# Loads of the later adaLN modulations: from SyncE's queue to GpSimd's, two tiles ahead of their sums, as one chain

## The chip, the cores and the metric

The kernel runs on one core of a Trainium2 chip. The metric is the device time of one execution in microseconds (us); a comparison goes by the median of several executions. Engines: PE is TensorE, DVE is VectorE, ACT is ScalarE, POOL is GpSimd, SP is SyncE, which here issues the transfers and computes nothing.

## The reference, cut to what matters

Two layers over x of 256 tokens and 2048 channels. A layer has a token mixer (a convolution module in layer 0, stick-breaking attention in layer 1) and then a gated feed-forward (ConvFFN) with 5632 hidden channels. Each of the four sub-layers has its own modulation from the conditioning vector c:

```python
def ada_ln(c, w, b):
    mod = jax.nn.silu(c) @ w + b
    shift, scale, gate = jnp.split(mod, 3, axis=-1)
...
shift, scale, gate = ada_ln(c, ffn_mod_w[i], ffn_mod_b[i])
h = rms_norm(x, ffn_norm_g[i]) * (1.0 + scale) + shift
x = x + gate * conv_ffn(h, ffn_up_w[i], ffn_dw_w[i], ffn_dw_b[i], ffn_down_w[i])
```

One modulation is a product of a vector with a 2048 x 6144 matrix, 48 MB of float32. Called by their names in the kernel they are mix0, ffn0 (layer 0), mix1 and ffn1 (layer 1). All is float32, and the output is the final RMS norm.

## The kernel before, in words

**Matrix products.** The weights come as a stream of raw tiles of 128 x 1024 float32 (512 KB, eight blocks of 128 x 128; the prediction calls one a piece), in the order in which TensorE uses them. ScalarE rounds a tile to its high half `wh`, VectorE subtracts to get the low half `wl` (`split_next`, lines 226 to 243), and TensorE makes three matmuls per block: wh with xh, wh with xl, wl with xh (lines 288 to 290). `raw` has 6 buffers, `wh` and `wl` 4 each. Raw tiles are loaded up to 5 pieces ahead, halves made up to 3 ahead (`look`).

**Order of the stages.** After the convolution module (pw1, pw2: 32 split pieces) the first ffn has the products up00a, up00b, up01a, down00, up01b and down01 with 8, 80, 4, 44, 84 and 44 pieces. Numbered through, the subtractions of pw2 are 1 to 32, up00a 33 to 40, up00b 41 to 120, up01a 121 to 124, down00 125 to 168, up01b 169 to 252, down01 253 to 296. Then come the attention's q, k and v products, the o product and the second ffn with the same products (688 pieces in all).

**Modulations.** A few are made on TensorE from rows, in the convolution module. The others go by tiles of 128 x 2048 (1 MB) that hold 128 rows of the transposed matrix: `mod_load` (309) takes one of the three buffers of `mraw` and issues the load, `mod_reduce` (314) multiplies it on VectorE with silu(c), held in `csr`, and sums along the rows into one column of `macc`, and `mod_sum` adds the bias. A part (shift 0, scale 1, gate 2) has 16 such tiles. `mods1` (985) makes the last part of ffn0, and mix1 and ffn1 whole: 7 parts, 112 tiles. It is a generator; `mod_part` (329) loads a tile, then sums the one before, and yields.

**What sets the order.** `tick` runs after every piece and advances `fill` at the rate of the stage (`RATES`: 0.25 steps a piece in up, 0.5 in down, 0.3 in the attention); `need` (344) runs it until a part is there. The program so recorded passes through a scheduler, which orders each engine's queue by what it expects to be ready. SP's loads are excepted from that:

```python
def load(src, dst):
    tc.keep_in_program_order(nc.sync.dma_start(dst, src))
```

so a load of a modulation holds its place among the loads of weights. Each engine takes its queue in order. GpSimd adds the squares for the rms (`sumsq`, 381), multiplies 10 of the 16 tiles at the entry of a sub-layer by 1/rms (408), and masks in the attention (1025, 1046).

Of the kernel before, what the change touches and what calls it, by code (L numbers as in the profile page):

```python
# [116 lines left out]
def hybrid_trunk(ctx: ExitStack, tc: tile.TileContext, cfg: Cfg, io: dict):  # L117
    nc = tc.nc
    D, T, H = cfg.D, cfg.T, cfg.H
    KD, KF, CW, FW = cfg.KD, cfg.KF, cfg.CW, cfg.FW  # L120
# [47 lines left out]
    def pc(name, i0=0, n=None):  # L168
        if name in cfg.ccols:
            t, (a, b) = cpar["t"], cfg.ccols[name]  # L170
        else:
            t, (a, b) = par, cfg.cols[name]
        return t[:, a:b] if n is None else t[:, a + i0:a + i0 + n]
# [41 lines left out]
    def load(src, dst):  # L215
        tc.keep_in_program_order(nc.sync.dma_start(dst, src))
# [84 lines left out]
    mt_at = {"mix0": list(range(2 * KD)), "ffn0": list(range(4 * cfg.rows0, KD)) + list(range(2 * KD, 3 * KD))}  # L301
# [4 lines left out]
    macc = const.tile([P, 3 * KD], F32, name="macc")  # L306
    moda, have, shift_ready = {}, set(), {}

    def mod_load(m, nb):
        v = mpool.tile([P, D], F32, name="mraw")  # L310
        load(io["mt_" + m][mt_at[m].index(nb) if m in mt_at else nb], v)
        return v

    def mod_reduce(m, nb, v):

        nc.vector.tensor_tensor_reduce(out=v, in0=v, in1=csr, scale=1.0, scalar=0.0, op0=ALU.mult, op1=ALU.add,  # L316
                                       accum_out=macc[:, nb:nb + 1])

    def mod_sum(m, nb, n):
        nc.vector.tensor_tensor(modv[m][:, nb:nb + n], macc[:, nb:nb + n], pc(bname[m], nb, n), op=ALU.add)  # L320

    def mod_scale(m, k0, n):

        if m not in moda:
            moda[m] = const.tile([P, KD], F32, name="a_" + m)
        nc.vector.scalar_tensor_tensor(moda[m][:, k0:k0 + n], modv[m][:, KD + k0:KD + k0 + n], 1.0,
                                       pc(gname[m], k0, n), op0=ALU.add, op1=ALU.mult)

    def mod_part(m, part, first=0, mark=True):
        ahead = []  # L330
        for nb in range(part * KD + first, (part + 1) * KD):
            ahead.append((nb, mod_load(m, nb)))
            if len(ahead) > 1:
                mod_reduce(m, *ahead.pop(0))
            yield
        mod_reduce(m, *ahead.pop(0))
        mod_sum(m, part * KD + first, KD - first)
        if part == 1:
            mod_scale(m, 0, KD)
        if mark:  # L340
            have.add((m, part))
        yield

    def need(m, *parts):
# [135 lines left out]
    with ExitStack() as cv:  # L480
# [105 lines left out]
                yield  # L586

        def mods0():
            part = mod_part("ffn0", 0, 4 * cfg.rows0, mark=False) if cfg.rows0 * 4 < KD else iter(())
            for _ in mod_rows():  # L590
                yield
                if ("ffn0", 1) in have and next(part, "end") != "end":
                    yield
            yield from part
            have.add(("ffn0", 0))
# [15 lines left out]
        def start_tile():  # L611

            kt = ready["k"]
            if kt == KD:
                return
            for nb in (KD + kt, kt):
                mod_reduce("mix0", nb, mod_load("mix0", nb))
                mod_sum("mix0", nb, 1)
            mod_scale("mix0", kt, 1)
            nc.scalar.activation(hf[kt], ys[kt], AF.Identity, bias=modv["mix0"][:, kt:kt + 1],  # L620
                                 scale=moda["mix0"][:, kt:kt + 1])
            ready["k"] += 1
# [144 lines left out]
        for i in range(KD * HEAD // PB):  # L767
            pw1_piece(next(pw1))
            if (i + 1) % (HEAD // PB) == 0:
                start_tile()  # L770
        fill.append(mods0())
        load_rows(1)
        look["load"], look["split"] = 5, 0
# [209 lines left out]
            gemm(f"down{i}1", gh, gl, down_done(1), quiet=QUIET)  # L983

    def mods1():
        yield from mod_part("ffn0", 2)
        for m, part in (("mix1", 1), ("mix1", 0), ("mix1", 2), ("ffn1", 1), ("ffn1", 0), ("ffn1", 2)):
            yield from mod_part(m, part)

    fill.append(mods1())  # L990
    entry1 = Entry("mix1")
    ffn(0, entry, entry1)
# [135 lines left out]
    for h in range(2):  # L1128
        t = slice(h * HT, (h + 1) * HT)
        nc.vector.reciprocal(rs[:, t], std[:, t])  # L1130
        v = mpool.tile([P, D], F32, name="mraw")[:, :KD * HT].rearrange("p (k t) -> p k t", k=KD)
# [129 lines left out]
```

## Time and profile before

| | |
|---|---|
| median of 3 executions | 2317.57 us (2312.26 to 2320.76) |
| the profiled execution | 2315.66 us, of which its span is 2313.9 |
| busy: PE, DVE, ACT, POOL | 2271.5, 1733.2, 1161.5, 263.8 us |
| HBM read | 598.58 MB, 260 GB/s over the span |

The span runs from the first to the last instruction that the profile shows; the rest of the execution lies around it. Busy time is time in which an engine had an instruction, overlaps counted once. Idle time in front of an instruction is put down to what ended it.

### The profile page before, as it was taken

The page shows a single profiled execution, that of the slowest core. Times are in us where ns is not written, and L with a number is a line of the kernel's source. Part 1 is how long each engine was busy: PE and PEld are TensorE (multiplying, and loading weights), DVE is VectorE, ACT ScalarE, POOL GpSimd, SP SyncE. Part 2 cuts the span into 40 slices and gives each one's busy share as a digit, 9 for nine tenths or more (in the row PEclk, how much of TensorE's full clock was granted, in tenths as well). Part 3 has the DMA queues.
Part 4 walks back from the last instruction along what each step waited for, and adds up shares of the span by engine and source line. Part 5 has one row for each costly group of instructions (what it writes and reads, how often), then busy time and mean ns, then how long its engine had stood idle before and what let it go on. Part 6 is the DMA issues. An engine that isn't in the chain of part 4 may idle for free.

```text
span 2313.9 us, 44108 instructions
## 1 busy us (share of the span) xinstructions
PE 2271.5 (98%) x17834; PEld 2167.5 (94%) x17834; DVE 1733.2 (75%) x2386; ACT 1161.5 (50%) x1776; POOL 263.8 (11%) x348
## 2 busy tenths in 40 slices
PE   7999999999999999999999999999999999999998
PEld 5888577999999999999999998999999999999997
DVE  7689967987888888888976676788876545666554
ACT  2056655754543355554465554647555434555543
POOL 4058601100000000001111100111000000000010
PEclk9999999999999999999999999999999999999999
DMA  9988679577789977788955667685775555555553
GB/s 397 417 326 302 255 303 406 204 280 286 276 323 363 346 284 257 289 297 315 349 190 196 244 241 268 211 289 183 289 245 188 189 186 190 186 189 191 185 190 110
DMA packets 139167, 603.56 MB, mean 261 GB/s; under 512 B 15441, under 2 KB 15569, under 8 KB 115153
## 3 DMA queue, kind: packets, MB, share of 16 engines
q1 hardware_dynamic: 138962, 600.74, 71.2%
q8 instruction: 139, 2.28, 0.4%
q14 instruction: 66, 0.54, 0.1%
HBM read 598.58 MB, written 2.10 MB: 260 GB/s over the span
## 4 chain that ended last, share of the span: by engine, by line
PE 81%; DMA 7%; DVE 7%; issue 2%; ACT 1%; POOL 0%; SPq 0%; DVEq 0%; ACTq 0%; POOLq 0%
PE ps L289 23%; PE ps L288 23%; PE ps L290 23%; PE ps L644 5%; DMA mraw<-in_mt_ffn 4%; DMA mraw<-in_mt_mix 3%; DVE wl L238 2%; DVE mraw L316 2%; PE auxa L559 2%; PE ps L1086 1%; PE ps L1087 1%; PE ps L1088 1%; DVE hl L363 0%; DVE t L947 0%; DVE hl L366 0%
## 5 line engine op out<-in xcount | busy, mean ns | idle before, releaser
L238 DVE TENSOR_TENSOR wl<-raw,wh 128x1024 fp32r<-128x1024 f32 x688 | 840.6, 1227 | 343.1 <-ACT wh L234 338.2
L234 ACT CAST wh<-raw 128x1024 fp32r<-128x1024 f32 x688 | 717.9, 1048 | 699.2 <-PE ps L289 543.4
L288 PE MATMUL ps<-hh,wh 128*128 128x256 f32 (+1 forms) x3264 | 915.7, 281 | 0.0
L289 PE MATMUL ps<-hl,wh 128*128 128x256 f32 (+1 forms) x3264 | 912.1, 279 | 0.0
L290 PE MATMUL ps<-hh,wl 128*128 128x256 f32 (+1 forms) x3264 | 908.4, 278 | 1.9 <-DVE wl L238 1.9
L289 PEld LDWEIGHTS ps<-hl,wh 128*128 128x128 f32 x3264 | 617.7, 189 | 0.3
L290 PEld LDWEIGHTS ps<-hh,wl 128*128 128x128 f32 x3264 | 612.6, 188 | 3.3 <-DVE wl L238 3.1
L288 PEld LDWEIGHTS ps<-hh,wh 128*128 128x128 f32 x3264 | 612.8, 188 | 0.3
L316 DVE CUSTOM_DVE_ANT_0 mraw<-mraw,csr 128x2048 f32<-128x2048 f32 x152 | 349.2, 2297 | 129.9 <-DMA mraw<-in_mt_ffn 82.3
L289 PE MATMUL ps<-gl,wh 128*128 128x256 f32 x1408 | 395.3, 281 | 0.0
L290 PE MATMUL ps<-gh,wl 128*128 128x256 f32 x1408 | 393.1, 279 | 1.1 <-DVE wl L238 1.1
L288 PE MATMUL ps<-gh,wh 128*128 128x256 f32 x1408 | 394.2, 280 | 0.0
L290 PEld LDWEIGHTS ps<-gh,wl 128*128 128x128 f32 x1408 | 264.7, 188 | 1.5 <-DVE wl L238 1.5
L289 PEld LDWEIGHTS ps<-gl,wh 128*128 128x128 f32 x1408 | 265.7, 189 | 0.0
L288 PEld LDWEIGHTS ps<-gh,wh 128*128 128x128 f32 x1408 | 264.9, 188 | 0.0
L381 POOL TENSOR_TENSOR sumsq<-sumsq,t 128x256 f32<-128x256 f32 x56 | 58.7, 1049 | 1584.0 <-ACT t L377 1583.7
L644 PE MATMUL ps<-hh,raw 128*128 128x256 f32 x832 | 188.8, 382 | 0.0
L644 PEld LDWEIGHTS ps<-hh,raw 128*128 128x128 f32 x832 | 157.8, 191 | 28.3 <-issue 5.8
L947 DVE SCALAR_TENSOR_TENSOR t<-ps,par,t 128x254 f32<-128x254 f32 x328 | 157.1, 479 | 4.1
L684 DVE SCALAR_TENSOR_TENSOR auxb<-u,cpar,auxb 128x256 f32<-128x256 f32 x297 | 121.6, 483 | 4.5 <-ACT auxb L668 3.7
L819 POOL TENSOR_TENSOR y<-y,hl 128x256 f32<-128x256 f32 x143 | 104.6, 732 | 13.2 <-ACT hl L693 3.0
L944 ACT ACTIVATE t<-ps,par 128x256 f32<-128x256 f32 x164 | 91.9, 560 | 1.9 <-PE ps L290 1.9
(232 smaller groups left out, 2201.6 us busy)
## 6 DMA issues: line engine op xcount, KB each, us to landing
raw<-in_w_down SPq DMA_DIRECT2D x176, 512.0 KB, 4.5
mraw<-in_mt_mix SPq DMA_DIRECT2D x80, 1024.0 KB, 7.7
mraw<-in_mt_ffn SPq DMA_DIRECT2D x72, 1024.0 KB, 7.5
raw<-in_w_pw SPq DMA_DIRECT2D x96, 512.0 KB, 8.4
raw<-in_w_up01b SPq DMA_DIRECT2D x84, 512.0 KB, 5.0
raw<-in_w_up11b SPq DMA_DIRECT2D x84, 512.0 KB, 4.4
raw<-in_w_up00b SPq DMA_DIRECT2D x80, 512.0 KB, 5.1
raw<-in_w_up10b SPq DMA_DIRECT2D x80, 512.0 KB, 4.4
```

Of the source, the lines that this page charges most:

```text
L234: nc.scalar.copy(wh[:, :n], v[:, :n])
L238: nc.vector.tensor_tensor(wl[:, :n], v[:, :n], wh[:, :n].bitcast(F32), op=ALU.subtract)
L288: nc.tensor.matmul(o, wh[:, c], xh[kt], start=first, stop=False, skip_group_check=halves > 0)
L289: nc.tensor.matmul(o, wh[:, c], xl[kt], start=False, stop=False, skip_group_check=halves > 0)
L290: nc.tensor.matmul(o, wl[:, c], xh[kt], start=False, stop=left[nb] == 0, skip_group_check=halves > 0)
L316: nc.vector.tensor_tensor_reduce(out=v, in0=v, in1=csr, scale=1.0, scalar=0.0, op0=ALU.mult, op1=ALU.add, accum_out=macc[:, nb:nb + 1])
L381: engine.tensor_tensor(self.sum, self.sum, sq, op=ALU.add)
L644: nc.tensor.matmul(banks[j][:, nb // KD * T:(nb // KD + 1) * T], w[:, b * P:(b + 1) * P], hf[kt], start=first, stop=left[j] == 0, skip_gro ...
L684: nc.vector.scalar_tensor_tensor(conv_ps[j], us[j % UBUFS][:, k:k + T], tap(j, k), conv_ps[j], op0=ALU.mult, op1=ALU.add)
L819: nc.gpsimd.tensor_tensor(ys[c], ys[c], pr, op=ALU.add)
L944: nc.scalar.activation(y, ps[:, :T], AF.Identity, bias=pc(f"fdb{i}", nb, 1), scale=w(FW - 1))
L947: nc.vector.scalar_tensor_tensor(y[:, s:], ps[:, :T - s], w(k), y[:, s:], op0=ALU.mult, op1=ALU.add)
```

## The change

`mods1` no longer goes part by part: it keeps one list over all 112 tiles, loads a tile, sums the oldest when three are held, so that two loads are ahead of the sums also over the ends of the parts, and makes the part's `mod_sum`, `mod_scale` and its entry in `have` at its last tile. Its loads are issued by GpSimd (`own=True`) and without `keep_in_program_order`. `mod_part` remains for the first part of ffn0, whose `have` entry `mods0` makes. Lines after 309 of the changed kernel are a little further down than before.

```diff
-    def mod_load(m, nb):
+    def mod_load(m, nb, own=False):
         v = mpool.tile([P, D], F32, name="mraw")
-        load(io["mt_" + m][mt_at[m].index(nb) if m in mt_at else nb], v)
+        src = io["mt_" + m][mt_at[m].index(nb) if m in mt_at else nb]
+        if own:
+            nc.gpsimd.dma_start(v, src)
+        else:
+            load(src, v)
         return v
...
-    def mod_part(m, part, first=0, mark=True):
+    def mod_part(m, part, first):
...
         mod_reduce(m, *ahead.pop(0))
         mod_sum(m, part * KD + first, KD - first)
-        if part == 1:
-            mod_scale(m, 0, KD)
-        if mark:
-            have.add((m, part))
         yield
...
     def mods1():
-        yield from mod_part("ffn0", 2)
-        for m, part in (("mix1", 1), ("mix1", 0), ("mix1", 2), ("ffn1", 1), ("ffn1", 0), ("ffn1", 2)):
-            yield from mod_part(m, part)
+        ahead = []
+
+        def finish():
+            m, part, nb, v = ahead.pop(0)
+            mod_reduce(m, nb, v)
+            if nb + 1 == (part + 1) * KD:
+                mod_sum(m, part * KD, KD)
+                if part == 1:
+                    mod_scale(m, 0, KD)
+                have.add((m, part))
+
+        for m, part in (("ffn0", 2), ("mix1", 1), ("mix1", 0), ("mix1", 2), ("ffn1", 1), ("ffn1", 0), ("ffn1", 2)):
+            for nb in range(part * KD, (part + 1) * KD):
+                ahead.append((m, part, nb, mod_load(m, nb, own=True)))
+                if len(ahead) > 2:
+                    finish()
+                yield
+        while ahead:
+            finish()
+            yield
```

The order of the built program, at three places. First GpSimd's queue from the squares of pw2 (`sumsq`) to the first masks of the attention; `t<-x,rstd` are the tiles multiplied by 1/rms, `mraw` the loads. Before:

```order
L381 TENSOR_TENSOR sumsq<-sumsq,t 128x256 x14
L408 TENSOR_TENSOR t<-x,rstd 128x256 x10
L381 TENSOR_TENSOR sumsq<-sumsq,t 128x256 x14
L408 TENSOR_TENSOR t<-x,rstd 128x256 x10
L1025 AFFINE_SELECT e<-e 128x128 x4
```

And now:

```order
L382 TENSOR_TENSOR sumsq<-sumsq,t 128x256 x13
L314 DMA mraw<-in_mt_ffn 128x2048 x2
L382 TENSOR_TENSOR sumsq<-sumsq,t 128x256
L314 DMA mraw<-in_mt_ffn 128x2048 x3
L409 TENSOR_TENSOR t<-x,rstd 128x256 x7
L314 DMA mraw<-in_mt_ffn 128x2048
L409 TENSOR_TENSOR t<-x,rstd 128x256 x3
L314 DMA mraw<-in_mt_ffn 128x2048 x10
L314 DMA mraw<-in_mt_mix 128x2048 x48
L314 DMA mraw<-in_mt_ffn 128x2048 x48
L382 TENSOR_TENSOR sumsq<-sumsq,t 128x256 x14
```

All 112 loads stand between the squares of pw2 and those of down01; each waits for the sum that frees its buffer, three tiles back.

Second, VectorE's queue in up00b: subtractions (`wl`), the taps of the short convolution (`t<-ps,par,t`), the gating (`t<-t,t`, `gl`), and a sum of a modulation, which is two rows (`mraw,macc` and the read of the accumulator, `macc`). Before:

```order
L316 ISA mraw_5103,macc_102<-mraw_5103,csr_83 128x2048
L316 ISA macc_102 128x1
L947 SCALAR_TENSOR_TENSOR t_5027<-ps_4969,par_84,t_5027 128x254
L238 TENSOR_TENSOR wl_5034<-raw_4963,wh_5033 128x1024
L947 SCALAR_TENSOR_TENSOR t_5027<-ps_4969,par_84,t_5027 128x255
L238 TENSOR_TENSOR wl_5065<-raw_4997,wh_5064 128x1024
L238 TENSOR_TENSOR wl_5109<-raw_5031,wh_5108 128x1024
L947 SCALAR_TENSOR_TENSOR t_5092<-ps_5037,par_84,t_5092 128x254
L947 SCALAR_TENSOR_TENSOR t_5092<-ps_5037,par_84,t_5092 128x255
L959 TENSOR_TENSOR t_5096<-t_5096,t_5092 128x256
L238 TENSOR_TENSOR wl_5140<-raw_5062,wh_5139 128x1024
L963 TENSOR_TENSOR gl8_5100<-t_5096,gh8_5099 128x256
```

The same pair of output blocks now:

```order
L321 ISA mraw_6150,macc_102<-mraw_6150,csr_83 128x2048
L321 ISA macc_102 128x1
L948 SCALAR_TENSOR_TENSOR t_5026<-ps_4968,par_84,t_5026 128x255
L238 TENSOR_TENSOR wl_5064<-raw_4996,wh_5063 128x1024
L238 TENSOR_TENSOR wl_5108<-raw_5030,wh_5107 128x1024
L948 SCALAR_TENSOR_TENSOR t_5091<-ps_5036,par_84,t_5091 128x254
L321 ISA mraw_6290,macc_102<-mraw_6290,csr_83 128x2048
L321 ISA macc_102 128x1
L948 SCALAR_TENSOR_TENSOR t_5091<-ps_5036,par_84,t_5091 128x255
L238 TENSOR_TENSOR wl_5139<-raw_5061,wh_5138 128x1024
L960 TENSOR_TENSOR t_5095<-t_5095,t_5091 128x256
L238 TENSOR_TENSOR wl_5173<-raw_5105,wh_5172 128x1024
```

Where one sum stood in four subtractions, two stand now, and the sums are of later tiles.

Third, VectorE's queue at the entry of ffn0, from the last tile of h (`hl`) to the first tiles modulated (`tm`, `t`) after the reciprocal that makes `rstd`. Before:

```order
L434 SCALAR_TENSOR_TENSOR hl_3695<-x,a_ffn_2873,hh_3694 128x256
L238 TENSOR_TENSOR wl<-raw,wh 128x1024 x4
L400 RECIPROCAL rstd<-t 128x256
L412 SCALAR_TENSOR_TENSOR tm<-x,a_ffn_2873,rstd 128x256
L238 TENSOR_TENSOR wl<-raw,wh 128x1024
```

And now:

```order
L446 TENSOR_TENSOR hl_3695<-v_ffn_99,hh_3694 128x2
L238 TENSOR_TENSOR wl<-raw,wh 128x1024 x3
L321 ISA mraw,macc<-mraw,csr 128x2048
L321 ISA macc 128x1
L401 RECIPROCAL rstd<-t 128x256
L238 TENSOR_TENSOR wl<-raw,wh 128x1024 x2
L413 SCALAR_TENSOR_TENSOR tm<-x,a_ffn_2873,rstd 128x256
```

A sum of the moved chain stands ahead of the reciprocal; another stands ahead of these rows, and a third behind them.

## Rows read from the trace of the kernel before

**Rows 1.** The page's first part: busy us (share of the span) xinstructions.
```profile
PE 2271.5 (98%) x17834; PEld 2167.5 (94%) x17834; DVE 1733.2 (75%) x2386; ACT 1161.5 (50%) x1776; POOL 263.8 (11%) x348
```

**Rows 2.** Windows: busy us of each engine with instructions, granted clock, DMA share, GB/s.
```profile
core 0: us, PE busy (x) PEld busy (x) DVE busy (x) ACT busy (x) POOL busy (x), PEclk, DMA share, GB/s
480.00:660.00 180.00, 179.46 (x1531) 178.85 (x1530) 149.77 (x196) 92.67 (x130) 0.00 (x0) 1.00 0.77 286
660.00:780.00 120.00, 120.00 (x1023) 120.00 (x1022) 101.24 (x107) 47.34 (x50) 0.00 (x0) 1.00 0.93 357
60.00:120.00 60.00, 57.62 (x261) 48.83 (x260) 39.69 (x56) 4.79 (x8) 0.00 (x0) 1.00 1.02 417
180.00:240.00 60.00, 60.00 (x295) 47.71 (x294) 58.03 (x146) 38.10 (x97) 51.13 (x72) 1.00 0.73 270
1080.00:1140.00 60.00, 60.00 (x512) 59.80 (x511) 57.70 (x59) 27.46 (x37) 9.77 (x8) 1.00 0.99 384
1740.00:1800.00 60.00, 60.00 (x516) 60.00 (x516) 40.18 (x55) 31.94 (x45) 0.00 (x0) 1.00 0.59 188
540.00:600.00 60.00, 59.46 (x504) 58.85 (x503) 49.97 (x65) 30.00 (x44) 0.00 (x0) 1.00 0.75 281
1020.00:1080.00 60.00, 58.87 (x501) 58.67 (x500) 49.16 (x72) 30.52 (x54) 4.63 (x4) 1.00 0.80 295
1620.00:1680.00 60.00, 58.98 (x505) 58.77 (x505) 50.22 (x66) 30.57 (x43) 0.00 (x0) 1.00 0.77 290
```

**Rows 3.** TensorE's waits: tile and line, releaser, us in total, times, longest us.
```profile
PE ps L290 <- DVE wl L238: 7.0, 9, 1.5
...
PE ps L288 <- ACT wh L234: 1.6, 1, 1.6
...
PE auxb L290 <- DVE wl L238: 1.1, 2, 0.7
```

**Rows 4.** VectorE's waits for the loads of modulations, same columns.
```profile
DVE mraw L316 <- DMA mraw<-in_mt_ffn: 82.3, 44, 4.0
DVE mraw L316 <- DMA mraw<-in_mt_mix: 47.4, 27, 3.0
```

**Rows 5.** Windows of the instructions on `mraw` alone: PE, PEld, DVE.
```profile
480.00:660.00 180.00, 0.00 (x0) 0.00 (x0) 36.68 (x16) 1.00 0.77 286
660.00:780.00 120.00, 0.00 (x0) 0.00 (x0) 42.14 (x19) 1.00 0.93 357
```

**Rows 6.** VectorE's timeline in up00b: start us, us, instruction [idle before].
```profile
641.32 2.29 DVE L316 CUSTOM_DVE_ANT_0 mraw<-mraw,csr 128x2048 f32<-128x2048 f32 x1 [2.16 <-DMA mraw<-in_mt_mix]
643.53 0.08 DVE L316 DVE_READ_ACCUMULATOR2_ANT macc<- 128x1 f32 x1
643.53 1.22 DVE L238 TENSOR_TENSOR wl<-raw,wh 128x1024 fp32r<-128x1024 f32 x1
...
650.87 2.29 DVE L316 CUSTOM_DVE_ANT_0 mraw<-mraw,csr 128x2048 f32<-128x2048 f32 x1 [0.49 <-DMA mraw<-in_mt_mix]
653.09 0.08 DVE L316 DVE_READ_ACCUMULATOR2_ANT macc<- 128x1 f32 x1
653.09 0.48 DVE L947 SCALAR_TENSOR_TENSOR t<-ps,par,t 128x255 f32<-128x255 f32 x1
653.48 1.22 DVE L238 TENSOR_TENSOR wl<-raw,wh 128x1024 fp32r<-128x1024 f32 x1
```

**Rows 7.** DMA issues: tile, queue, operation, count, KB each, median us to landing.
```profile
mraw<-in_mt_ffn SPq DMA_DIRECT2D x72, 1024.0 KB, 7.5
raw<-in_w_up00b SPq DMA_DIRECT2D x80, 512.0 KB, 5.1
```

**Rows 8.** Timelines of VectorE and GpSimd at the entry of ffn0.
```profile
404.04 2.28 DVE L316 CUSTOM_DVE_ANT_0 mraw<-mraw,csr 128x2048 f32<-128x2048 f32 x1
...
421.28 1.75 DVE L400 RECIPROCAL rstd<-t 128x256 f32<-128x256 f32 x1
...
423.17 5.11 POOL L408 TENSOR_TENSOR t<-x,rstd 128x256 f32<-128x256 f32 x5 [13.64 <-DVE rstd L400]
```

More of the change, by code (lines that the diff above doesn't have):

```diff
@@ L588, in mods0 @@
         def mods0():
-            part = mod_part("ffn0", 0, 4 * cfg.rows0, mark=False) if cfg.rows0 * 4 < KD else iter(())
+            part = mod_part("ffn0", 0, 4 * cfg.rows0) if cfg.rows0 * 4 < KD else iter(())
             for _ in mod_rows():
```

## The prediction

> **What bounds the kernel now.** I read the page's first part, the table of windows, the waits of TensorE, one stretch of VectorE's timeline, and last the order of the built program, since the diff doesn't say where the moved loads come to stand.
>
> TensorE is busy for 98% of the span [rows 1]. A *piece* is one raw tile of weights: 8 blocks, so 24 matmuls. In a stretch without any modulation (1740 to 1800 us) 516 matmuls run in 60 us, with the granted clock at 1.00 as in all these rows (the upper level, 2.4 GHz) [rows 2]: 60 / 516 x 24 = 2.79 us a piece. In the down products it is 120 / 1023 x 24 = 2.81 us [rows 2]. With modulations beside them the up products still run 1531 matmuls in 180 us, 510 per 60 us [rows 2]. So the modulations are nearly hidden already, and whatever shortens their waits alone can win little.
>
> How little: of TensorE's waits on VectorE's low halves and ScalarE's high halves the view lists 7.0 + 1.6 + 1.1 = 9.7 us in the whole program, and some of that lies in stretches that the change doesn't touch [rows 3]. From the other side, three stretches with modulations lack 12, 15 and 11 matmuls against 516 [rows 2], 38 x 0.116 = 4.4 us. VectorE's own idle time for those loads, 82.3 + 47.4 us [rows 4], looks like the prize but isn't: it is idle time of an engine with room.
>
> How much room decides the case. In the up products VectorE is busy 149.77 us of 180, of which the 16 sums take 36.68 [rows 2, 5]. The rest is 113.1 us over 1531 / 24 = 63.8 pieces: **1.77 us a piece**. In the down products it is (101.24 - 42.14) / (1023 / 24) = **1.39 us a piece** [rows 2, 5]. One sum holds VectorE 2.21 us: it starts at 641.32 and the next subtraction at 643.53 [rows 6]. So in an up product there is room for (2.79 - 1.77) / 2.21 = 0.46 sums a piece, in a down product for 0.64. Before, the paced chain uses 0.25 and 0.5.
>
> **The change part by part.** 112 loads of 1 MB leave SP's queue for GpSimd's. SP loads were held in program order, so those of the modulations stood among the weights at the paced places and their sums followed. GpSimd's are not held, and the built program shows what the scheduler made of it: all 112 stand ahead of the mix1 entry's squares. The 112 sums on VectorE come between the 32nd and the 246th subtraction: 3 at the entry to ffn0, 36 + 2 in the rest of up00b and in up01a (74 pieces), 30 in down00 (44 pieces), 41 in up01b (78 pieces). Before, the same chain ran from the 51st to the 478th, into the attention and the o product. So the pace is now 0.52 sums a piece in up and 0.68 in down, both **above VectorE's room**, and its queue is in order: what stands ahead of a subtraction delays it.
>
> *Up, 152 pieces with 79 sums.* VectorE needs 152 x 1.77 + 79 x 2.21 = 269 + 175 = 444 us; TensorE needs 152 x 2.79 = 424. With VectorE fully used: +20 us. With the fill of the densest full-clock stretch of the trace, 58.03 of 60 us [rows 2], 444 / 0.967 = 459: +35. I take 20, because the timeline of an up product shows no hole between a sum, the tap and the next subtraction (650.87, 653.09, 653.48) except where it waits for data [rows 6]. The low end is 0, if non-sum work in a queue that is never idle shrinks by the 0.13 us a piece that are lacking.
>
> *Down00, 44 pieces with 30 sums.* VectorE: 44 x 1.39 + 30 x 2.21 = 127.5 us against 44 x 2.81 = 123.6, so +4. The bytes press harder: 44 raw tiles of 512 KB and 30 of 1024 KB [rows 7] are 23.1 + 31.5 = 54.5 MB. At 417 GB/s, the fastest row, that takes 131 us; at 384, the fastest with a full TensorE beside it [rows 2], 142. So +7 to +18, and 0 below if more than 417 can be had. I take +7: 417 was reached, and 384 was all that was asked for in that row. By the Trainium skill ("DMA: Bandwidth & Descriptors", Specifications) HBM gives one core about 358 GB/s. By that figure down00 would take 152 us and this term would be an estimated +29; both rows of the trace are above it, so the measurement decides.
>
> *Entry to ffn0.* Two sums now stand ahead of the reciprocal of the rms, and a third among the modulated tiles. VectorE works there without a hole from the last old sum (404.04) to the reciprocal (421.28), and GpSimd's modulations have waited 13.64 us for it [rows 8]. Three sums are 6.6 us. TensorE's waits in this region were small but present (0.7 us at most on auxb) [rows 3], with some two pieces of subtractions in hand, so part is absorbed. Bounds 0 and 6.6 plus 2 for a first load not landed; I take +5.
>
> *Afterwards.* No modulation remains in down01, the attention and o. That gives back the lost matmuls and waits: between 4.4 and 9.7 us; I take -8, nearer to the waits view, since it counts every wait of the program and the lacking matmuls are those of three stretches alone.
>
> *At nothing:* SP's 112 issues, on a queue that only issues; the three short sums at the ends of parts, kept as they were; on GpSimd, the issue of a load, whose price no row shows. GpSimd has nothing to do in the ffn products (0.00 busy) [rows 2], which covers up to 5.8 us each (the distance of two sums). If that cover fails, the next sum is late by the difference. GpSimd's queue waits: the sixth load waits for the third sum while three modulated tiles stand behind it, which down the line feed up00b's third piece; part of the entry term. The mix1 squares and the attention's masks stand behind the 112th load, which is out by the 244th subtraction, while down01 begins at the 252nd: no wait.
>
> Sum: 20 + 7 + 5 - 8 = **+24 us**. The profiled execution took 2315.66 us, so 2339.7; the median of the runs is 1.9 us higher, 2317.57, which gives **2341 us**, 1.0% slower.
>
> **The rivals.**
> *The packing costs what it gives back (same).* If VectorE fits (0 for up), down00 costs 4 and the entry 2, less 8: -2, some 2316 us; with half of up, 2326. For: the overload in up is only 4.7%, and TensorE's lead of subtractions smooths it. Against: the lead is a few pieces and the overload lasts 152.
> *Faster.* The waits for loads vanish (two tiles in hand, no weights ahead in the queue), and VectorE keeps the 2.79 us. It decides at 1.64 us of other work a piece in up instead of 1.77. Then everything in the waits view goes, and the lacking matmuls come back: 2317.6 - 9.7 - 4.4 = 2303 us. For: VectorE's 129.7 us of idle time [rows 4]. Against: that idle time is exactly the room that the denser sums use up.
> *Weights starve in down00 (much slower).* Rows of a raw tile are 4 KB, of a modulation 8 KB, from the sizes [rows 7]. If two queues alternate by such rows, weights get a third of 417 GB/s, 139, while loads of modulations are outstanding: 0.524 MB / 139 = 3.77 us a piece, 44 x 3.77 = 166 instead of 131, +35 more: 2376 us. The same size comes from late landings: a sum every 4.1 us with three buffers leaves 3 x 4.1 - 2.2 = 10.1 us from issue to landing; at twice the 7.5 us of today [rows 7] the sums come every 5.7 us, 30 of them 172 us, +41: 2382 us. In up it needs 14.7 us, so it bites in down00 alone. The Trainium skill ("DMA: Bandwidth & Descriptors", Queues, rings and completion order) says that each engine takes turns between queues packet by packet, which is this rival's rule; with one queue in use, no row here shows it.
> *The change doesn't do what it says:* two tiles of lead is what it writes, but the order shows a lead without the pace. That is my forecast, not a rival.
>
> **How the numbers follow.** Within 0.5% of 2317.6 means 2306 to 2329, about what a measurement can tell from no change. The forecast has 0.62: its own range is 2327 to 2360, from all low ends at once (13 + 4 + 2 - 10 = +9; 13 is two thirds of the term for up) to some three quarters of all high ends (35 + 18 + 7 - 5 = +55). Starvation has 0.12, the same case 0.19, faster 0.07. Slower: 0.59 + 0.12, since a little of the forecast lies under 2329: 0.71. Same: 0.19 + 0.03 = 0.22. Faster 0.07. The range for 8 in 10 takes the forecast, the upper half of the same case and most of starvation: 2318 to 2376.
>
> **What would show it.** Right: in the windows from about 470 to 1020 us VectorE at 57 us of 60 or more, TensorE's count at 490 to 500 per 60 us in place of 510, its waits on the low halves of the weights tens of us in total; down00 near 417 GB/s; sums gone after about 1050 us, and counts of 516 there. Wrong: a full 516 in up with VectorE under 57 us (the non-sum work shrank), or VectorE idle for loads through the packed stretch, with landings over 10 us (starvation).

## The result and the profile after

The change costs 0.2%: 2325.13 us, median of 22 runs (2319.68 to 2328.38), against 2319.50 us of the kernel before, median of 22 runs beside them (2312.26 to 2325.13). The medians are 5.6 us apart; the ratio is 1.002 [1.0012, 1.0028], which is +4.6 us, clear of noise but within the 0.5% that the prediction calls no change. The forecast was 2341 us and slower. The profiled execution took 2326.32 us with a span of 2324.6, 10.7 us longer than the span of before. 6.0 us of that are not of the change, as the table below shows.

The first part of the page and the DMA issues show what moved. The columns of the second fence are tile, queue, operation, count, KB each, median us to landing.

```profile
PE 2279.0 (98%) x17834; PEld 2172.8 (93%) x17834; DVE 1731.9 (75%) x2386; ACT 1162.6 (50%) x1776; POOL 319.7 (14%) x460
```
```profile
mraw<-in_mt_ffn POOLq DMA_DIRECT2D x64, 1024.0 KB, 8.1
...
mraw<-in_mt_mix POOLq DMA_DIRECT2D x48, 1024.0 KB, 7.8
...
raw<-in_w_up00b SPq DMA_DIRECT2D x80, 512.0 KB, 6.5
```

The same 17834 matmuls, the same 2386 instructions of VectorE, and 112 more of GpSimd, which are the 112 loads [rows 1]. A load of ffn's modulations lands 8.1 us after its issue instead of 7.5, a tile of up00b's weights 6.5 us instead of 5.1 [rows 7].

The windows show where time was lost and won (busy us of each engine with its instructions, granted clock, DMA share, GB/s). First the kernel after:

```profile
285.00:300.00 15.00, 15.00 (x101) 8.96 (x97) 7.10 (x15) 5.66 (x11) 0.00 (x0) 0.80 0.31 103
360.00:375.00 15.00, 12.31 (x75) 9.05 (x74) 10.91 (x12) 5.67 (x9) 2.25 (x3) 0.77 1.00 412
435.00:450.00 15.00, 11.59 (x90) 11.18 (x89) 15.00 (x21) 11.30 (x25) 9.79 (x9) 0.93 0.51 179
480.00:660.00 180.00, 180.00 (x1546) 180.00 (x1545) 180.00 (x229) 92.97 (x128) 16.95 (x32) 1.00 0.98 376
660.00:780.00 120.00, 119.80 (x1021) 119.63 (x1020) 118.17 (x127) 47.67 (x53) 13.86 (x27) 1.00 1.01 401
840.00:1020.00 180.00, 179.36 (x1534) 179.07 (x1533) 180.00 (x229) 90.65 (x129) 16.93 (x32) 1.00 0.98 380
1080.00:1140.00 60.00, 60.00 (x514) 60.00 (x513) 38.35 (x42) 30.74 (x44) 10.16 (x10) 1.00 0.58 186
```

Then the two of before that stood nowhere yet:

```profile
285.00:300.00 15.00, 15.00 (x124) 10.74 (x128) 8.96 (x18) 7.93 (x13) 0.00 (x0) 1.00 0.53 196
360.00:375.00 15.00, 12.25 (x95) 9.69 (x95) 11.56 (x13) 7.69 (x11) 1.81 (x2) 1.00 1.02 419
```

Read the row of 480 to 660 first. VectorE is busy for 180.00 of 180 us, which was foretold, and TensorE runs 1546 matmuls in it, the full rate, which was not: 15 more than before [rows 2]. Then the first two rows: in these stretches both kernels run the same instructions, since the first moved load is issued at 409.74 us; yet the granted clock is 0.80 and 0.77 of full speed after, and 1.00 before.

**A table of losses.** Both traces record all 17834 matmuls, in nearly one order. So the start of the k-th matmul in a run, less the start of the k-th before, is how far the run is behind at that place, and the growth of this number over a stretch is what the stretch lost. This is worked out from the traces for the profiled execution of every run of this study (us; stretches by the times of before; 0.52 and the like are explained with the runs; the last column leaves out what was lost ahead of 400 us):

```
                     to 400  400-450 450-660 660-900 900-1020 1020-1100 1100-end | behind 400
after                   6.0     5.6    -1.6     7.1      0.1      -1.8     -4.9  |   4.6
e1_sp_queue             5.7     0.0     1.9     1.2      0.0      -1.4     -1.6  |   0.1
e2_held                 4.2    -0.1    -1.6     0.0      0.0       1.0      3.9  |   3.3
e5_late_start           0.2     4.4    -1.6     7.2      1.3      -1.8     -4.9  |   4.8
e3_held_up052          -0.2    -0.1    -1.1    11.0      2.6      -1.8     -4.9  |   5.7
e4_held_up065           0.0    -0.1    22.2    12.7      9.7      -1.8     -4.9  |  38.0
e6_half_sums            6.4    -0.1    -1.6     2.7      0.0      -1.8     -5.0  |  -5.7
e7_three_held           5.8    -0.1    -1.6     7.7      1.5       2.1     -5.0  |   4.6
e8_held_046             4.3    -0.1    -1.6     0.0      0.0       4.2     -3.3  |  -0.8
e9_none_in_down01       4.0    -0.1    -1.6     0.0      0.0      -1.8     -5.0  |  -8.5
e10_none_sp             0.7     0.0    13.5    21.7     12.9       0.5     -5.0  |  43.5
```

The column "to 400" is no work of the change: it is the fall of the granted clock to its lower level (0.5, 1.2 GHz) for 3.4 or 6.8 us near 284 and 366 us, in some executions and not in others. The two rows of after give (1 - 0.80) x 15 + (1 - 0.77) x 15 = 6.5 us of lost full speed for the 6.0 in the table. The last column of after, 4.6 us, is what the ratio says too. So it is the one to explain: entry to ffn0 +5.6, up00b and up01a -1.6, down00 and the start of up01b +7.1, the rest of up01b +0.1, and -6.7 from 1020 us on. The cut at 900 us hides where the 7.1 fall: counted by matmuls, down00's 44 pieces lose 2.3 us and up01b's 84 lose 4.9, 3.8 of them in its first 12.

Three views show the three places. First VectorE's timeline of the kernel after in up00b (start us, us, instruction):

```profile
603.16 2.33 DVE L321 CUSTOM_DVE_ANT_0 mraw<-mraw,csr 128x2048 f32<-128x2048 f32 x1
605.37 0.13 DVE L321 DVE_READ_ACCUMULATOR2_ANT macc<- 128x1 f32 x1
605.37 0.47 DVE L964 TENSOR_TENSOR gl<-t,gh 128x256 fp32r<-128x256 f32 x1
605.71 0.53 DVE L948 SCALAR_TENSOR_TENSOR t<-ps,par,t 128x254 f32<-128x254 f32 x1
606.10 1.27 DVE L238 TENSOR_TENSOR wl<-raw,wh 128x1024 fp32r<-128x1024 f32 x1
607.23 0.53 DVE L948 SCALAR_TENSOR_TENSOR t<-ps,par,t 128x255 f32<-128x255 f32 x1
607.62 1.27 DVE L238 TENSOR_TENSOR wl<-raw,wh 128x1024 fp32r<-128x1024 f32 x1
608.76 2.34 DVE L321 CUSTOM_DVE_ANT_0 mraw<-mraw,csr 128x2048 f32<-128x2048 f32 x1
...
614.35 2.34 DVE L321 CUSTOM_DVE_ANT_0 mraw<-mraw,csr 128x2048 f32<-128x2048 f32 x1
```

From 603.16 to 614.35 there are four subtractions (L238, one a piece) and two sums, without a hole: 11.19 us for four pieces, where TensorE needs 4 x 2.79 = 11.17. Each subtraction is 1.27 us long, but the next instruction starts 1.13 us behind its start; a tap (L948) is 0.53 long and the next starts 0.39 later; a sum 2.33 long and 2.21. In the queue of before, with idle time in it, the taps often stood two together:

```profile
629.54 0.99 DVE L947 SCALAR_TENSOR_TENSOR t<-ps,par,t 128x254 f32<-128x254 f32 x2
630.45 2.35 DVE L238 TENSOR_TENSOR wl<-raw,wh 128x1024 fp32r<-128x1024 f32 x2
```

There a pair takes 0.91 us from its start to the next instruction; apart, the two take 2 x 0.39 = 0.78.

Second, the entry to ffn0, in VectorE's timeline and in TensorE's [the last bracket: idle us before it, and what ended it]:

```profile
427.25 2.28 DVE L321 CUSTOM_DVE_ANT_0 mraw<-mraw,csr 128x2048 f32<-128x2048 f32 x1
429.46 0.08 DVE L321 DVE_READ_ACCUMULATOR2_ANT macc<- 128x1 f32 x1
429.46 1.75 DVE L401 RECIPROCAL rstd<-t 128x256 f32<-128x256 f32 x1
...
440.40 2.28 DVE L321 CUSTOM_DVE_ANT_0 mraw<-mraw,csr 128x2048 f32<-128x2048 f32 x1
...
443.48 3.34 DVE L367 SCALAR_TENSOR_TENSOR hl<-t,v_ffn,hh 128x256 fp32r<-128x256 f32 x3
446.74 1.74 DVE L238 TENSOR_TENSOR wl<-raw,wh 128x1024 fp32r<-128x1024 f32 x1
```
```profile
445.13 0.29 PE L289 MATMUL auxb<-hl,wh 128*128 128x256 f32 x1
448.54 0.58 PE L290 MATMUL auxb<-hh,wl 128*128 128x256 f32 x1 [3.12 <-DVE wl L238]
```

The reciprocal comes at 429.46 instead of 421.28 [rows 8], the third sum stands at 440.40 in front of the low halves of the first tiles, and TensorE waits 3.12 us for the subtraction that follows them, up00b's first (a wait on this tile, `auxb`, in which the first products there are summed, took at most 0.7 us before [rows 3]). Its clock falls at 448.0 us, inside that wait, for 3.4 us.

Third, down00. ScalarE now waits for weights to land (tile, releaser, us in total, times, longest us; from 660 to 850 us), which it did not before:

```profile
ACT wh L234 <- DMA raw<-in_w_down: 41.2, 19, 2.7
...
ACT wh L234 <- DMA raw<-in_w_up01b: 16.0, 8, 2.7
```

and the tiles of weights in these 190 us land in 12.8 us in the median, against 6.3 before. First after, then before:

```profile
DMA to landing us min/median/max: 5.5/12.8/17.1
```
```profile
DMA to landing us min/median/max: 3.5/6.3/9.0
```

**The lead.** The traces also give how far VectorE is ahead of TensorE: the time from the end of a subtraction to the start of the first matmul that uses it. While there is lead, VectorE can be late without a loss. Its mean over stretches of subtractions, by their numbers (up00b is 41 to 120, down00 125 to 168, up01b 169 to 252), worked out as the table above, in us:

```
                    51-60  111-120  125-135  158-168  169-178  239-248
before                3.3      4.9      5.2      5.9      5.7      6.0
after                 4.9      3.0      3.8      0.8      0.5      1.1
e3_held_up052         5.5      1.0      2.2      0.6      1.0      1.0
e4_held_up065         3.1      0.9      2.7      5.9      4.4      6.2
e6_half_sums          5.9      6.0      6.0      1.5      0.9      5.8
e9_none_in_down01     5.1      4.0      4.8      5.9      5.7      2.5
```

In the kernel after, up00b spends 1.9 us of lead that no count of matmuls shows, down00 nearly all of the rest, and up01b runs without any to speak of.

### The profile page after: what moved, and what is told of

Read it like the earlier page. It is cut to its first block, busy times and chain, and to the rows that moved or that the text cites. A ratio compares the mean times of both kernels' runs of the same rounds, so it can differ in the third digit from the quotient of the medians.

```text
span 2324.6 us, 44213 instructions
## 1 busy us (share of the span) xinstructions
PE 2279.0 (98%) x17834; PEld 2172.8 (93%) x17834; DVE 1731.9 (75%) x2386; ACT 1162.6 (50%) x1776; POOL 319.7 (14%) x460
## 4 chain that ended last, share of the span: by engine, by line
PE 84%; DVE 8%; DMA 5%; issue 2%; ACT 1%; SPq 0%; DVEq 0%; POOL 0%; ACTq 0%
PE ps L288 24%; PE ps L289 23%; PE ps L290 23%; PE ps L645 5%; DVE mraw L321 3%; DMA mraw<-in_mt_mix 3%; DVE wl L238 2%; PE auxa L560 2%; PE ps L1105 1%; PE ps L1106 1%; PE ps L1107 1%; DVE t L948 1%; DMA raw<-in_w_up01b 1%; DMA raw<-in_w_down 1%; PE auxb L1106 0%
## 5 line engine op out<-in xcount | busy, mean ns | idle before, releaser
L238 DVE TENSOR_TENSOR wl<-raw,wh 128x1024 fp32r<-128x1024 f32 x688 | 846.3, 1235 | 428.6 <-ACT wh L234 424.0
L948 DVE SCALAR_TENSOR_TENSOR t<-ps,par,t 128x254 f32<-128x254 f32 x328 | 161.1, 491 | 3.7 <-ACT t L945 0.7
```

Of the source, the lines that this page charges most:

```text
L238: nc.vector.tensor_tensor(wl[:, :n], v[:, :n], wh[:, :n].bitcast(F32), op=ALU.subtract)
L948: nc.vector.scalar_tensor_tensor(y[:, s:], ps[:, :T - s], w(k), y[:, s:], op0=ALU.mult, op1=ALU.add)
```

## The experiments

Two questions stood at the start: which of its parts (the queue, the floating of the sums, the pace) makes the time, and at what pace VectorE becomes the bound. Diffs are against the changed kernel unless another is named. In the table above each has its line. "Held" means that a sum is kept in program order, so that the pace table RATES places it again and the scheduler doesn't; the loads stay on GpSimd's queue, two tiles ahead.

**e1_sp_queue: the chain and the two tiles of lead, on SP's queue.**
```diff
-                ahead.append((m, part, nb, mod_load(m, nb, own=True)))
+                ahead.append((m, part, nb, mod_load(m, nb)))
```


> The changed kernel with its 112 loads back on SP's queue, two tiles ahead and as one chain; the order of the sums is then nearly that of the kernel before (first at the 51st subtraction, last at the 454th). Theory (the packed stretch is free in up; the loss is 5.6 us of sums at the entry of ffn0 and 7.2 us of bytes in down00, against 8 us of waits for loads removed): no entry loss, no loss in down00, and the waits for loads of VectorE (129.7 us before) shrink to under a half; 0 to 8 us faster than before, ratio 0.9965 to 1.000. Rival (issuing from GpSimd costs by itself): the same ratio here, 0.9965 to 1.000, and the cost appears in e2_held.

Measured: 2322.59 us (12 runs), ratio 1.0012 [1.0003, 1.0021]. With SP's queue, where `load` holds them in program order again, the sums come back to the paced places, and entry and down00 lose next to nothing (0.0 and 1.2 us). But the gain isn't there either: 1.9 us are lost from 450 to 660, those and the 1.2 mostly at 641 to 684 us, and little is won later. That the two tiles of lead gain by themselves is not borne out.

**e2_held: GpSimd's queue, the sums at the paced places.**
```diff
-    def mod_reduce(m, nb, v):
+    def mod_reduce(m, nb, v, held=False):
-        nc.vector.tensor_tensor_reduce(
+        ins = nc.vector.tensor_tensor_reduce(
...
+        if held:
+            tc.keep_in_program_order(ins)
-            mod_reduce(m, nb, v)
+            mod_reduce(m, nb, v, held=True)
```


> The changed kernel with each moved sum held behind what VectorE was given before it, so that loads go by GpSimd's queue but sums keep the pace of 0.25 and 0.5 a piece (first at the 60th subtraction, last at the 465th). Theory: no sums at the entry, down00 at about 355 GB/s and with no loss, waits for loads gone: 4 to 8 us faster than before, ratio 0.9965 to 0.998. Rival (GpSimd's queue costs by itself): as slow as the change or slower, 1.002 to 1.006, with the loss spread over the whole stretch.

Measured: 2321.24 us (12 runs), 1.0001 [0.9991, 1.001]; a gain was expected and isn't there. Its line tells more than its median: from 400 to 1020 us it loses nothing and wins 1.6, so the queue and the two tiles of lead by themselves cost nothing and end the waits of up. What it wins there it loses from 1020 us on, where its sums still stand in down01, the attention and o: waits of TensorE in down01, and 6.1 us in one stretch of o, with a wait of 2.1 us and a fall of the clock behind it. The second part is that of the one profiled execution.

**e5_late_start: the first load held behind the entry.**
```diff
+            ins = nc.gpsimd.dma_start(v, src)
+            if (m, nb) == ("ffn0", 2 * KD):
+                tc.keep_in_program_order(ins)
...
+            if i == 0:
+                fill.append(mods1())
...
-    fill.append(mods1())
```


> The changed kernel with its first load held behind GpSimd's work at the entry of ffn0, so that one sum stands there (at the 42nd subtraction) in place of three; the rest is packed as in the change and ends at the 249th. Theory: the 5.6 us at the entry go, down00 still loses about 7 us: 4 to 6 us faster than the change, ratio to before 0.9995 to 1.000. Rival (the entry's loss comes from something else there, such as the clock): as slow as the change, 1.002.

Measured: 2323.82 us (12 runs), 1.001 [0.9999, 1.0022]. The entry still loses 4.4 us, though a single sum stands there now instead of three: TensorE waits 3.6 us on the same tile auxb.

```profile
PE auxb L290 <- DVE wl L238: 3.6, 1, 3.6
```

So most of the loss is not that of the three sums together but of the one just ahead of up00b: it stands between the entry's last products and the first subtractions, where the lead falls to 0.1 us in every run, that of before too.

**e7_three_held: the first three sums held, the rest as changed.** The edit is that of e2, with
```diff
+            mod_reduce(m, nb, v, held=m == "ffn0" and nb < 2 * KD + 3)
```


> The changed kernel with the sums of its first three tiles held behind what VectorE was given before them; their loads stay at the entry, and the packing begins at the 60th subtraction. Theory (the three sums at the entry cost the 5.6 us): no loss from 404 to 455 us, down00 as in the change; 4 to 7 us faster than the change, ratio to before 0.999 to 1.0005. Rival (the loads by GpSimd's queue there, or GpSimd's tiles behind them, cost it): TensorE still loses over 3 us between 404 and 455 us.

Measured: 2323.98 us (11 runs), 1.0014 [1.0001, 1.0027]. The loads are issued at the entry as in the changed kernel, the sums are not there, and the loss of 5.6 us is gone (-0.1). TensorE's waits from 404 to 455 us in both, first after, then e7:

```profile
PE auxb L290 <- DVE wl L238: 3.1, 1, 3.1
PE ps L290 <- DVE wl L238: 2.4, 2, 1.3
```
```profile
PE ps L290 <- DVE wl L238: 1.1, 1, 1.1
PE auxb L290 <- DVE wl L238: 0.7, 1, 0.7
```

So the sums make the entry's loss, and neither the loads nor GpSimd's queue do. The forecast of the time was missed all the same, since the end of the chain moved on: five sums now stand in down01, which lost 2.1 us instead of winning 1.8 (a wait of 2.2 us with a fall of the clock behind it), and 660 to 1020 us lost 2.0 us more.

**e3_held_up052: e2 with the packed pace.** The pace that the scheduler made, written into the table:
```diff
-... "up": (0.25, 0.25), "down": (0.5, 0.0), ... "up00b": (0.27, -1.5)
+... "up": (0.52, 0.25), "down": (0.68, 0.0), ... "up00b": (0.52, -1.5)
```


> As e2_held, with rates of 0.52 in up and 0.68 in down, the density of the change, from the 52nd subtraction on; no sum at the entry. Theory: in up no loss over 3 us (VectorE needs 11.2 us per four pieces, TensorE 11.17), in down00 +6 to +9 us, afterwards gains: ratio 0.9985 to 1.0005. Rival (the scheduler's own places are what makes the dense sums fit): in up over 10 us lost, 1.004 or more.

Measured: 2326.60 us (10 runs), 1.0024 [1.0014, 1.0034], above the forecast and about the time of the changed kernel, with the same pattern: nothing lost in up00b and up01a (-1.1), 11.0 us from 660 to 900, 2.6 in the rest of up01b, 6.7 won later. So the pace makes the time, whoever sets it. That up00b loses nothing isn't the whole of it: its lead falls from 5.5 to 1.0 us there.

**e4_held_up065: e2 with a pace that must be too much.**
```diff
-... "up": (0.25, 0.25), ... "up00b": (0.27, -1.5)
+... "up": (0.65, 0.25), ... "up00b": (0.65, -1.5)
```


> Sums held as in e2_held, at 0.65 a piece in up (45 in the 70 last pieces of up00b, 42 in the 64 first of up01b) and 0.5 in down00. Theory (at the change's 0.52 VectorE's full queue needs 11.2 us per four pieces, just what TensorE needs): 2.6 sums per four pieces need 6.8 + 5.7 = 12.5 us against 11.17, so up loses (70 + 64) / 4 x 1.3 = 45 us, less 8 us of gains: +30 to +45 us, ratio 1.013 to 1.02. Rival (VectorE had room to spare in up at 0.52): under +10 us.

Measured: 2356.09 us (4 runs), 1.0162 [1.0145, 1.0178]. Here VectorE is the bound, and its trace measures its need: from the start of the 51st subtraction to that of the 121st it takes 222.9 us, 2.5 of them idle, with 45 sums. (222.9 - 2.5 - 45 x 2.21) / 70 = **1.73 us a piece** beside the sums. TensorE's loss of 22.2 us over the same 70 pieces gives a little less, (195.4 + 22.2 - 45 x 2.21) / 70 = 1.69, where 195.4 is 70 x 2.79, because VectorE spent its lead first. The window of up00b:

```profile
480.00:660.00 180.00, 166.56 (x1368) 161.76 (x1367) 178.27 (x220) 82.07 (x113) 19.60 (x37) 1.00 0.98 379
```

VectorE is 99% busy, where the changed kernel has 100%, but TensorE runs 1368 matmuls instead of 1546. The busy share can't tell the two apart.

**e6_half_sums: e3 with sums of half the width**, so the second half of each of the 112 moved rows is left out of its sum. The loads stay whole.
```diff
+        w = D // 2 if held else D
-... out=v, in0=v, in1=csr,
+... out=v[:, :w], in0=v[:, :w], in1=csr[:, :w],
```


> e3_held_up052 with each moved sum over only the first 1024 of a row's 2048 columns (the other half of those modulations is left out); the loads and their places stay. Theory (bytes bound down00): VectorE is relieved by about 1.1 us a sum and down00 with the start of up01b still loses 6 us or more against the kernel before, at 395 to 405 GB/s. Rival (VectorE bounds down00): the loss there falls under 3 us.

Measured: 2316.42 us in a single execution, beside 2318.94 of before (median of 22); one time is no verdict, and the stretches are what counts. From 660 to 900 us it loses 2.7 us, where e3 loses 11.0 with the same bytes. Windows of 20 us, first the kernel after, then e6:

```profile
760.00:780.00 20.00, 20.00 (x173) 20.00 (x172) 18.81 (x19) 6.76 (x7) 2.21 (x5) 1.00 1.02 415
780.00:800.00 20.00, 19.20 (x163) 18.97 (x162) 19.51 (x19) 7.17 (x7) 2.53 (x5) 1.00 1.02 415
800.00:820.00 20.00, 18.64 (x154) 18.03 (x154) 17.92 (x20) 6.50 (x7) 2.65 (x5) 1.00 1.02 416
```
```profile
780.00:800.00 20.00, 20.00 (x173) 20.00 (x172) 13.01 (x20) 7.28 (x7) 2.64 (x5) 1.00 1.02 415
800.00:820.00 20.00, 18.97 (x158) 18.36 (x156) 11.17 (x13) 7.18 (x8) 1.07 (x2) 1.00 1.01 412
```

Both move 412 to 416 GB/s at a DMA share of 1.01 to 1.02. With half sums the shortage of bytes costs TensorE 2.7 us, all at the start of up01b, under the 3 us that the rival had set. But it also eats lead: 6.0 us at the start of down00, 0.9 behind it. So by an estimate from these two the shortage of bytes delays the halves by 5.1 + 2.7 = 7.8 us, and how much of it TensorE feels depends on the lead in hand. Half sums had kept that lead in up00b, where e3 had spent its own (1.0 us at the end) and the kernel after a part of it (3.0). The run relieves VectorE in both places at once, so how the loss divides between bytes and VectorE's load stays open: one makes the other worse.

**e8_held_046: e2 with the pace of the predicted room.**
```diff
-... "up": (0.25, 0.25), ... "up00b": (0.27, -1.5)
+... "up": (0.46, 0.25), ... "up00b": (0.46, -1.5)
```


> Sums held as in e2_held, at 0.46 a piece in up and 0.5 in down, from the 54th subtraction to the 289th: under VectorE's room in up, under the bytes' limit in down00, none in the attention. Theory: no loss at the entry, in up or in down00, and the later gains of 5 to 8 us: ratio 0.9965 to 0.9985, faster than both kernels. Rival (dense loads cost wherever they stand): no faster than before, 0.9995 or more.

Measured: 2318.22 us (11 runs), 0.9995 [0.9984, 1.0007]. Nothing is lost from 400 to 1020 us; VectorE is 175.73 of 180 us busy from 840 to 1020. But 19 sums are left over for down01 and cost 4.2 us there (1020 to 1100), with a fall of the clock at 1077.5 us.

**e9_none_in_down01: e2 with a pace under the limit, and no sums where they cost.** 33 sums in up00b, 22 in down00, 40 in up01b and 4 at the seams of these, none in down01, the attention and o, and the last 13 in up10b.
```diff
-... "up": (0.25, 0.25), "down": (0.5, 0.0), "qk": (0.3, 0.0), "v": (0.3, 0.0),
-... "o": (0.45, -3.0), ... "up00b": (0.27, -1.5), ... "qk0b": (0.3, -1.5)
+... "up": (0.48, 0.25), "down": (0.5, 0.0), "down01": (0.0, 0.0), "down10": (0.0, 0.0), "qk": (0.0, 0.0), "v": (0.0, 0.0),
+... "o": (0.0, 0.0), ... "up00b": (0.48, -0.5)
```


> Sums held, loads by GpSimd's queue; 0.48 a piece in up, 0.5 in down00, two sums in down01, none in the attention and o, the last 13 in up10b. Theory (nothing lost below VectorE's room and the bytes' limit; e8_held_046 lost its gain in down01 alone): no loss at the entry, in up00b to up01b under 1 us, then gains of 1.5 us in up00b, 1.8 in down01, 3.5 in the attention: 5 to 8 us faster than before at the same clock drops, ratio 0.9965 to 0.9985. Rival (the gains belong to the lead, not to where the sums stand): no better than e8_held_046, 0.9995.

Measured: **2311.82 us** (11 runs), 0.9961 [0.9948, 0.9974]: faster than the kernel before by 0.4%, clear of noise though under the 0.5% of the forecast's bound, and so faster than the change. It loses nowhere behind 400 us and wins 8.5.

```profile
480.00:660.00 180.00, 180.00 (x1545) 180.00 (x1545) 178.36 (x226) 93.48 (x128) 16.48 (x31) 1.00 0.96 367
660.00:780.00 120.00, 120.00 (x1024) 120.00 (x1023) 108.57 (x114) 48.66 (x52) 11.16 (x21) 1.00 0.98 381
```

**e10_none_sp: e9 with the loads on SP's queue**, held in program order there as in e1.
```diff
-                ahead.append((m, part, nb, mod_load(m, nb, own=True)))
+                ahead.append((m, part, nb, mod_load(m, nb)))
```


> e9_none_in_down01 with the loads on SP's queue. Theory that the queue doesn't matter and the places of the sums do: within 1.5 us of e9_none_in_down01 in the stretch from 450 to 1460 us. Rival (on SP's queue a load that waits for its buffer holds the weights behind it): 2 to 6 us more than e9_none_in_down01, in waits of TensorE for low halves between 450 and 1050 us.

Measured: 2364.32 us (5 runs), 1.0196 [1.0172, 1.022]. That is 52.5 us above e9, far more than either side had thought of. What SP waits for from 455 to 1050 us (its DMA queue's own waits), first e9, then e10, with TensorE's waits of e10 in the same stretch behind:

```profile
SPq L216 <- DVE wl L238: 407.0, 172, 6.7
```
```profile
SPq L216 <- DVE macc L321: 411.5, 88, 11.0
```
```profile
PE ps L290 <- DVE wl L238: 28.5, 45, 3.1
```

In e9 SP waits for a subtraction to free a buffer of weights, which is its normal pace. In e10 it stands up to 11.0 us on a load of a modulation that waits for a sum to free its buffer, and the loads of weights stand behind it in the same queue; TensorE loses 48.1 us from 450 to 1020 us. At about the pace of before (e1) this costs some 3 us, at about twice the pace some 50. This is what GpSimd's queue buys. The Trainium skill ("DMA: Bandwidth & Descriptors", Issuing engines are not separate DMA queues) says that issuing from several engines only saves the sequencer's time for issuing, which is usually small. For the bytes the trace agrees: both queues together moved 417 GB/s at most, as one did [rows 2]. For the time it doesn't: what was saved here is a queue's wait for a buffer.

## Why the prediction was wrong

**What bounds the kernel: right.** TensorE with its pace of 2.79 us a piece is the bound, and in up VectorE is the next; e4 shows it as the bound.

**Where the sums go: right.** 33, 27 and 33 sums are in the windows of 480 to 660, 660 to 780 and 840 to 1020 us, the places that the order of the program had shown.

**Up, +20 us: the step that failed.** "VectorE needs 152 x 1.77 + 79 x 2.21 = 269 + 175 = 444 us; TensorE needs 152 x 2.79 = 424. With VectorE fully used: +20". Measured: nothing lost in up00b and up01a (-1.6 us, which belongs to the gains), and 4.9 us in up01b, some of it owed to the tiles that down00 left late (e6 loses 2.7 at the same place). The sum's 2.21 us was taken from start to start, and it held. The 1.77 us was taken from busy time in a queue with idle time in it, where an instruction in front of a gap counts in full, also the tail that the next one would run beside if it were already waiting. In a full queue the same work takes (11.19 - 2 x 2.21) / 4 = 1.69 us a piece by the timeline of after, and 1.70 over the 60 pieces between the starts of the 60th and the 120th subtraction (170.4 us with 31 sums); its window gives 1.66, (180 - 33 x 2.21) / (1546 / 24), with one sum cut by its edge, and e4 gives 1.73. A good part is the taps: 0.91 us a pair, 0.78 when something stands between them. With 1.70 the term would have been 152 x 1.70 + 175 - 424 = +9, and what is left of it above the measured 4.9 is about the lead that was spent (4.9 us in up00b's first pieces, 1.1 at up01b's end). The prediction had weighed that lead and put it aside ("the lead is a few pieces and the overload lasts 152"), which is fair against 20 us and not against 9. The low end had the other half as its condition ("if non-sum work in a queue that is never idle shrinks by the 0.13 us a piece that are lacking"): it shrank by 0.07 to 0.11 in the kernel after, and by 0.04 in e4. The choice of 20 between 0 and 35 was the mistake, since "no hole" in a timeline shows that instructions follow each other, not that their lengths add. The Trainium skill ("Perfetto Trace Analysis", Optimizing Scalar/DVE Operations) says that an instruction's profiled latency holds a part that overlaps with the next instruction. The trace agrees: 0.12 to 0.14 us of each subtraction, tap and sum in the timeline of after. Small as it is, over the 152 pieces it took about half of the term.

So VectorE was full, as foretold, and TensorE was full too, a pair that neither sign of the prediction had. The kernel after stands just over the line between the two, since its lead shrinks in up00b; e9 at 0.48 sums a piece lies about on it, e4 at 0.65 far over.

**Down00, +7: right as a delay, not as a loss.** 417 GB/s was reached and held: 414 to 417 in every window of 20 us from 720 to 840. The 358 GB/s of the Trainium skill ("DMA: Bandwidth & Descriptors", Specifications) were again not the limit. The 7.1 us of the table look like the term, but only 2.3 of them fall on down00's pieces; most of the loss comes after 780 us, when down00's last pieces and up01b's first run on late tiles. By the estimate from e6 the bytes delay the halves by 7.8 us, which is the term; the lead of 3.8 us that stood at down00's start hid a part of that, which the term hadn't thought of, and what was lost beyond the rest goes with the full VectorE. That the two met at 7.1 is luck.

**Entry, +5: right (5.6), with another weight.** Of three sums the last does most of the harm (e5, one sum, 4.4 us; e7, none, -0.1). Besides TensorE's wait of 3.1 us there was the fall of the clock behind it, which no term held.

**Afterwards, -8: right.** -1.8 and -4.9 us in the stretches that the term names, and -1.6 in up00b, make -8.3 us; e9, which has these gains and no loss, wins 8.5.

**At nothing:** the issue of a load on GpSimd is 16.95 / 32 = 0.53 us, well inside the 5.8 that were covered. VectorE's waits for the moved loads from 404 to 1100 us are two lines of 0.8 and 0.3 us:

```profile
DVE mraw L321 <- DMA mraw<-in_mt_mix: 0.8, 3, 0.4
DVE mraw L321 <- DMA mraw<-in_mt_ffn: 0.3, 1, 0.3
```

So the change does what it says, and most of the 129.7 us of VectorE's idle time [rows 4] is gone; it was room, and nothing that TensorE had waited for.

**The rivals.** *Same* happened: its condition, up at 0, was nearly met (4.9 us), with a dearer entry than it had (5.6 instead of 2). *Faster* was decided at 1.64 us, and the measured 1.69 and 1.70 lie above that line; it took e9 to get there, by taking the sums away from the entry, thinning those of down00 and moving the line: at 0.48 sums a piece it is 2.79 - 0.48 x 2.21 = 1.73. Its 2303 us were too low besides, since they added 9.7 and 4.4 us, two views of the same waits. *Starvation* didn't happen: 44 tiles of down00 were issued from 665.1 to 789.4 us, 2.89 us a piece instead of 3.77, and modulations in that stretch landed in 9.0 us in the median and 9.9 at most, just under the 10.1 at which it would have bitten. By the places where they fell, the losses are 5.6 at the entry, 2.3 in down00 and 4.9 in up01b, less 8.3: +4.5, where 5, 7 and 20 less 8 were forecast. The time lay in the range of 2318 to 2376 us; the chance of 0.71 on slower rested on the term for up.

**What stays open.** Why the scheduler's free placement came to stand just at VectorE's limit wasn't tried. How the 7.2 us of down00 and up01b divide between late tiles and VectorE's load isn't known. Nor is it known what decides in which executions the clock falls near 284 and 366 us.

## What to carry to other kernels

Room on an engine that is nearly full is to be measured from start to start in the densest stretch, not by adding busy time of a sparse one: 0.07 us a piece made +20 of what would have been +9. A lead in hand hides part of an overload and of a shortage of bytes alike, and is spent without a trace in the count of matmuls, so it belongs into the sum. Work that hides beside a bound belongs where there is room, under the limit, and not in a stretch where a second resource is full (down00's bytes) or where no lead is left (just ahead of up00b); in e9 the same sums at better places gave 0.4% against the kernel before. And a load that must wait for a buffer should not stand in the queue that feeds the bound.

## What the runs showed of the hardware

- The granted clock fell to 0.5 in or just behind some short waits of TensorE: at 448.0 us in a wait of 3.1 us, at 447.1 in e5 after 3.6, at 1483.8 in e2 after one of 2.1. Such a wait costs more than its length: about 1.7 us more for 3.4 us at half speed. Not every wait does it: one of 2.1 us at 849 us in e10 had no fall behind it. Waits of 2.0 and 1.65 us near 284 and 365 us stand in all twelve traces; the clock fell behind both in seven of the eleven later profiles and not in the others, nor in that of before, which alone makes spans differ by up to 6.4 us. A pair of profiles is therefore compared by stretches, not by ends.
- A load of 1 MB through GpSimd's queue landed in 7.8 to 8.1 us in the median in the kernel after, through SP's in 7.5 before [rows 7], with other traffic beside it.
- One core's DMA engines moved 414 to 417 GB/s for 120 us on end (720 to 840 us of the kernel after), with TensorE 93 to 100% and VectorE 90 to 99% busy beside them.
